# A streaming conformer encoder layer in float32: depthwise taps tied behind softmax minima, input rows asked for earlier, two FFN products exchanged, outputs on another DMA queue

## The chip, the cores and the metric

The kernel runs on one core of one Trainium2 chip. The metric is the device time of one execution in microseconds; the kernel before has a median of 3021.13 us over three runs. Five engines work side by side, each through its own instructions in their order: TensorE (PE) multiplies matrices and transposes, VectorE (DVE) and ScalarE (ACT) do elementwise work, GpSimd (POOL) some more of it, and SyncE (SP) issues nearly all DMA transfers. ACT can issue DMAs too, on a queue of its own.

## The reference, cut to what matters

A prompt of 2048 rows and a sample of 64 rows, each row 1024 wide, pass through one layer. All is float32.

```python
h = rms_norm(x, norm1_g) * (1 + sc1) + sh1
glu_a, glu_b, q, k, v, g_conv, g_attn = split(h @ w_in)
u = glu_a * sigmoid(glu_b)
conv_out = silu(layer_norm(depthwise_conv31(u) + b_dw)) @ w_conv_out
q, k = rms_norm(q), rms_norm(k)                # per head, 8 heads of 64
o = softmax(q @ k.T / 8 + bias, banded) @ v    # own chunk of 64 and 8 chunks before
merged = sigmoid(g_conv) * conv_out + sigmoid(g_attn) * (o @ w_attn_out)
x = x + gt1 * (merged @ w_o)
gate, up = split((rms_norm(x, norm2_g) * (1 + sc2) + sh2) @ w_ffn_in)
y = x + gt2 * ((silu(gate) * up) @ w_ffn_out)
```

The depthwise convolution has 31 taps per channel and reads the 30 rows before. Rows of u, k and v are returned as states too.

## The kernel before, in words

Every float32 product is made of three matmuls on halves of the operands: a high part (`whi`, `hh`) that ACT copies out and a low part (`wlo`, `hl`) that DVE or POOL makes by a subtraction.

**First phase: four row blocks.** The 2112 rows are worked in blocks of 576, 512, 512 and 512 rows (`PBLOCKS`, line 34). The table `ORDER` (line 536) gives each block eight stages: `q`, channel tile 0, `k`, tile 1, `v`, tiles 2 and 3, and the sixteen gate columns `g`. A channel tile is one call of `glu` (line 1174): PE makes two products, 48 matmuls of 512 columns in the last three blocks, ACT takes a tanh, and DVE writes `u`. Then `convolve` (line 1202) runs its 31 taps over that tile on DVE: one `tensor_scalar` with the bias, and thirty `scalar_tensor_tensor`, all writing the same `y`, so that each follows the one before. When the four tiles are through, `conv_norm` (line 1221) normalises over channels: POOL sums the four tiles into `s`, PE multiplies `s` by a matrix of ones, and DVE, ACT and POOL share the rest.

Attention of a block begins two model microseconds after its `v` stage and goes on beside tiles 2 and 3, the gates and the next block's first stages. Each head (`attend`, line 1412) makes four score tiles `sc` on PE, one per 128 rows. There is one buffer for `sc` (tag `s`, `bufs=1`; in the first block two score tiles share it, one in each half). So PE can start a score tile only when `softmax_max` (line 1314) has read the one before: that is one DVE instruction which adds the bias and takes the row minimum of the negated scores (`pr`, with its result in `sm`). ACT makes the exponentials, PE transposes them (`ptp`), ACT and DVE split them (`ph`, `pl`), and PE multiplies by v (`po`).

The next block's rows are prepared in the same phase: `norm_tile` (line 1109) loads 128 rows as `x_t`, ACT squares them, POOL takes the power, DVE scales, PE transposes (`pt<-ident,x_t`), DVE applies the modulation, and ACT and DVE write `hh` and `hl`, which the next block's products read. The generators of the four tiles are put in their lane at the twelfth gate (`NORM_G` = 11), two at a time. There are three `x_t` buffers, in a pool that also holds the rows of v on their way out.

**What sets the order.** All steps are generators in lanes (`Lane`, line 108), emitted along a model of each engine's load (`Stream`, line 161). What is emitted then goes through the framework's scheduler, which reorders each engine's instructions by readiness in a time model of its own. `issue_after(ins)` forbids it to place an instruction ahead of `ins` on the same engine.

**Second phase: merge and FFN**, in three row blocks of 576, 768 and 768 (`CBLOCKS`, line 35). The FFN's first product runs as seven half-size products per column group `f`, a recursive scheme with sums of weights and sums of activations; `up_operands` (line 540) lists the weights' order and `up` (line 1962) issues the products. The products named `s2` and `s1` go into the same PSUM bank `y`, and between them ACT must copy the bank to `u` (`u2`). In the last two row blocks the FFN's second product is cut into four parts per pair of `f` (`down_pair`, line 1938), put between the products at the places that `dn_at` (line 548) gives; in the first row block `down` (line 2022) runs between two products of every even `f`. The last `down` of a row block makes the outputs `acc`, which leave by `nc.sync.dma_start`, so on SP's queue, behind which the next row block's gate columns (`tg<-g_d`) are loaded.

Of the kernel before, what the change touches and what calls it, by code (L numbers as in the profile page):

```python
# [44 lines left out]
TURN_LAG = 2500.0  # L45
KN_LAG = 5000.0
X_LAG = 8000.0
ON_POOL = ()
DMA_LAG = 4000.0
OUT_LAG = 4000.0  # L50
# [2 lines left out]
SIDE_G = 10  # L53
SPLIT_G = 2
NORM_G = 11
NORM_W = 2
SCORE_ROOM = {"dve": 2500}
TURN_NS = 600.0
# [481 lines left out]
def up_operands(f):  # L540

    ops = (["s2", "s3", "s1"] if f else ["s3", "s2", "s1"]) + ["a12"] * (f >= EARLY) + ["a22"] + ["a11"] * (EARLY <= f + 1 < NF) + ["s4"]
    return [(f + (op == "a11"), op) for op in ops]


def dn_at(f):

    return (0, 1, 3, 6 if f == PAIRS[-1] else 4)  # L550


def mod_order():
# [34 lines left out]
def streaming_layer(ctx: ExitStack, tc: tile.TileContext, I, O):  # L588
# [512 lines left out]
    def square(x_t, n):  # L1101
# [4 lines left out]
        dve.tensor_tensor(ssq[:n, 0:1], ssq[:n, 0:1], ssq[:n, 1:2], ALU.add)  # L1106
        return rsqrt_mean(wk, ssq[:n, 0:1], n, 1, D)

    def norm_tile(lo, t, free):

        c = slice(t - lo, t - lo + P)
        x_t = load_x(t, P, wa, "x", 3)
        yield stream.load["pe"] + X_LAG
        r = square(x_t, P)
        yield stream.when("pool")
        dve.tensor_scalar(x_t, x_t, r, None, ALU.mult)
        yield stream.when("dve") + PE_LAG
        for g in range(2):
            pt = ps_g.tile([P, 4, P], F32, tag="gp", name="pt")
            h = temp("h32", (P, 4, P))  # L1120
            for k in range(4):
                pe.transpose(pt[:, k], x_t[:, (4 * g + k) * P : (4 * g + k + 1) * P], ident)
            stream.after("dve", "pe")
            for k in range(4):
                kk = 4 * g + k
                dve.tensor_scalar(h[:, k], pt[:, k], A1[:, kk, 0:1], B1[:, kk, 0:1], ALU.mult, ALU.add)
            yield stream.when("dve")
            yield lambda: free["columns"] >= c.stop
            f = slice(4 * g, 4 * g + 4)
            act.activation(hh[:, f, c], h, AF.Copy)  # L1130
            yield stream.when("act")
            dve.tensor_tensor(hl[:, f, c], h, hh[:, f, c].bitcast(F32), ALU.subtract)
# [66 lines left out]

    now = {"scored": -1, "finished": -1, "bias": None}  # L1200

    def convolve(u, y, ct, b):
        w = UW if b == 0 else HIST + QB
        n = w - HIST
        states = [(cs_s, HIST + SMP)] if b == 0 else [(cs_p, w)] if b == len(PBLOCKS) - 1 else []
        if states:
            yield stream.when("dve") + TURN_LAG
        for rows_, e in states:
            pt = ps_g.tile([P, 512], F32, tag="gp", name="pt")
            pe.transpose(pt[:HIST, :P], u[:, e - HIST : e], ident)  # L1210
            s = wa.tile([HIST, P], F32, tag="cc", name="cc", bufs=2)
            dve.tensor_scalar(s, pt[:HIST, :P], 0.5, None, ALU.mult)
            stream.at(stream.when("dve"), lambda s=s, rows_=rows_: nc.sync.dma_start(rows_[:, ct * P : (ct + 1) * P], s))
            yield
        gps.tensor_copy(hist[:, ct], u[:, w - HIST : w])
        dve.tensor_scalar(y[:, ct, :n], u[:, :n], wd[:, ct, 0:1], bdw[:, ct : ct + 1], ALU.mult, ALU.add)
        for k in range(1, TAPS):
            dve.scalar_tensor_tensor(y[:, ct, :n], u[:, k : k + n], wd[:, ct, k : k + 1], y[:, ct, :n], ALU.mult, ALU.add)
            yield

    def conv_norm(y, c0, n, t0):
        yv = y[:, :, c0 : c0 + n]
        yield lambda: not conv.gens
        s = wk.tile([P, 512], F32, tag="ln_s", bufs=1)

        def total():
# [311 lines left out]
    for b, stage in ORDER:  # L1538
        lo, hi = PBLOCKS[b]
        if stage == "q":  # L1540
            free, ahead = {"columns": 0}, {}
            if b + 1 < len(PBLOCKS):
                ahead = {t: norm_tile(hi, t, free) for t, _ in token_tiles(*PBLOCKS[b + 1])}
        if stage == "q" and b == 0:
            pass
        elif stage in ("q", "k", "v"):
            qkv(b, "qkv".index(stage), norms)
            if stage == "v":

                def heads(b=b):  # L1550
                    work.drain()
                    stream.flush()
                    attention(b)
                    if b == 3:
                        attn.burst, attn.spacing = 2, 0.0

                stream.at(stream.load["pe"] + HEADS_NS, heads)
        elif stage == "g":
            for g in gates(b, free):
                if g == NORM_G:  # L1560
                    for gen in ahead.values():
                        norm_lane.add(gen)
                if g == SIDE_G and b == len(PBLOCKS) - 1:
                    work.drain()
                    conv.drain()
                    stream.flush()
                    side.close()
                    wc = ctx.enter_context(tc.tile_pool(name="wc", bufs=1, side="right"))
                    cs = tile_chunks(*CBLOCKS[0])[0]
                    src = load_mixed(*cs, 0)  # L1570
                    first_gates = gate_columns(*cs, 0)
            norms = ahead
        else:
# [173 lines left out]
    for s, (lo, hi) in enumerate(CBLOCKS):  # L1747
# [208 lines left out]
        def rest_of_late(n=99):  # L1956
            while late and n:
                n -= 1
                if next(late[0], None) is None:
                    late.pop(0)  # L1960

        def up(f, ops, at):
# [25 lines left out]
            v = half_piece(1, "v")[:, :half]  # L1988
            keep(v, z)
            rest_of_late()  # L1990
            if f % 2 == 0:
                at(0)
            step(y, "s1", "t1", False, False)
            plus(v, y, v)
            if f % 2:
                at(4)
            if f >= EARLY:
                x = bank("gp")
                step(x, "a12", "b21", True, True)
                plus(x, x, s1)  # L2000
                silu(c1, x)
            if f % 2 == 0:
                at(1)
            step(z, "a22", "t4", False, True)
            plus(z, z, u2)
# [16 lines left out]
        def down(fs, ws):  # L2022

            last = fs[-1] == NF - 1
            for i, (t, n) in enumerate(tiles):
# [19 lines left out]
                for j, ps in enumerate(pss):  # L2045
# [9 lines left out]
                    else:  # L2055
                        if not final:
                            dve.tensor_tensor(ps[:m], ps[:m], both, ALU.add)
                        if n < m:
# [5 lines left out]
                        dve.tensor_tensor(dst, ps[:n], dst if final else x1[j], ALU.add)  # L2064
                        stream.at(
                            stream.when("dve") + OUT_LAG,
                            lambda t=t, n=n, f=f, dst=dst: nc.sync.dma_start(rows(y_p, y_s, t, n)[:, f], dst),
                        )
            for _ in fs:
                W.done()  # L2070
# [91 lines left out]
```

## Time and profile before

| | |
|---|---|
| median of three runs | 3021.13 us (3019.73 to 3027.58) |
| the profiled execution | 3021.16 us |
| its span, first to last instruction | 3018.7 us |
| mean granted TensorE clock | 0.987 of full speed |
| PE, DVE, ACT, POOL busy | 96%, 67%, 44%, 32% of the span |
| DMA moved | 690.95 MB, mean 229 GB/s |
| row blocks of the first phase end at about | 345, 640, 930 and 1222 us |
| merge and FFN, three row blocks, end at about | 1735, 2377 and 3019 us |

The time of an execution lies about 2.5 us over its span. A wait is told as who sat idle, for how long, and whose result ended it. Instructions of the kernel's engines all carry line 103, which is the recording helper, so they are told apart by the tiles that they write and read: `sc` are scores, `sm` the minima and sums, `y<-u,wd,y` a tap, `ps` a product's bank.

### The profile page before, as it was taken

How to read it: one execution, taken by the hardware profiler on the slowest of the kernel's cores; microseconds unless marked ns; L12 is line 12 of the kernel's file. 1: busy time of each engine (PE TensorE's matmuls, PEld its weight loads, DVE VectorE, ACT ScalarE, POOL GpSimd, SP SyncE). 2: the span in 40 equal slices, each digit the busy share in tenths (PEclk: the TensorE clock that was granted, in tenths of full speed). 3: DMA queues.
4: the chain of work that ended last, by engine and by line, in shares of the span. 5: the costliest groups of instructions: out<-in, count | busy, mean ns of one | idle time of the engine just before them, and what ended most of it. 6: DMA issues, size and time to landing. Idle time of an engine off the chain costs nothing. (4 is left out here: it accounts for less than half of the span.)

```text
span 3018.7 us, 44690 instructions
## 1 busy us (share of the span) xinstructions
PE 2912.8 (96%) x16199; PEld 2600.1 (86%) x16199; DVE 2019.5 (67%) x3647; ACT 1324.5 (44%) x2375; POOL 956.4 (32%) x599
## 2 busy tenths in 40 slices
PE   7989898999999999999999999999999999999998
PEld 4889776888878788888999989999999898999997
DVE  5896687657966895577766755556565757366567
ACT  3334542563355256464444335434444244333331
POOL 1200120101011101355467323157766331333331
PEclk9999999999999999999999999999999999999999
DMA  9888888887987789886444786446556965355554
GB/s 301 266 279 284 264 293 292 265 255 259 305 273 223 254 284 295 256 295 235 149 146 155 240 286 223 151 141 202 194 170 212 352 206 188 116 168 175 168 163 174
DMA packets 487018, 690.95 MB, mean 229 GB/s; under 512 B 38421, under 2 KB 316809, under 8 KB 486798
## 3 DMA queue, kind: packets, MB, share of 16 engines
q1 hardware_dynamic: 474517, 670.72, 67.8%
q10 hardware_dynamic: 12280, 17.39, 1.6%
q8 instruction: 127, 2.08, 0.3%
q14 instruction: 94, 0.76, 0.1%
HBM read 503.79 MB, written 184.19 MB: 228 GB/s over the span
## 5 line engine op out<-in xcount | busy, mean ns | idle before, releaser
L103 POOL TENSOR_TENSOR wlo<-wst,whi 128x1024 fp32r<-128x1024 f32 (+1 forms) x171 | 388.1, 2274 | 495.3 <-ACT whi L103 448.5
L103 PE MATMUL ps<-t,whi 128*128 128x384 f32 (+1 forms) x2112 | 507.2, 324 | 12.4 <-DVE t L103 5.5
L103 PE MATMUL pd<-whi,hid 128*128 128x512 f32 x1356 | 439.7, 391 | 3.4 <-DVE acc L103 3.4
L103 ACT ACTIVATE whi<-wst 128x1024 fp32r<-128x1024 f32 (+1 forms) x272 | 265.7, 980 | 346.2 <-PE ps L103 117.3
L103 PEld LDWEIGHTS ps<-t,whi 128*128 128x128 f32 x2112 | 371.4, 189 | 21.2 <-DVE t L103 6.4
L103 PE MATMUL ps<-b,whi 128*128 128x384 f32 (+1 forms) x1584 | 379.9, 325 | 1.9 <-DVE pt L103 1.6
L103 DVE SCALAR_TENSOR_TENSOR y<-u,wd,y 128x512 f32<-128x512 f32 (+1 forms) x480 | 369.0, 773 | 8.2
L103 PE MATMUL ps<-hh,whi 128*128 128x512 f32 (+2 forms) x992 | 363.1, 366 | 0.3 <-DVE pl L103 0.3
L103 PE MATMUL ps<-hl,whi 128*128 128x512 f32 (+2 forms) x992 | 345.7, 348 | 0.0
L103 PE MATMUL ps<-hh,wlo 128*128 128x512 f32 (+2 forms) x992 | 345.7, 348 | 0.0
L103 PE MATMUL ps<-t,wlo 128*128 128x384 f32 (+1 forms) x1056 | 341.0, 323 | 0.0
L103 DVE TENSOR_TENSOR acc<-acc,pd 128x512 f32<-128x512 f32 x440 | 289.7, 683 | 69.8 <-PE pd L103 65.9
L103 PEld LDWEIGHTS pd<-whi,hid 128*128 128x128 f32 x1356 | 254.5, 188 | 57.8 <-DVE acc L103 6.5
L103 PEld LDWEIGHTS ps<-b,whi 128*128 128x128 f32 x1584 | 277.0, 189 | 4.9 <-DVE pt L103 2.0
L103 PE MATMUL pd<-wlo,hid 128*128 128x512 f32 x700 | 273.7, 391 | 0.0
L103 PE MATMUL ps<-b,wlo 128*128 128x384 f32 (+1 forms) x792 | 256.3, 324 | 0.0
L103 ACT ACTIVATE pr<-pr,sm 128x640 f32<-128x640 f32 (+3 forms) x272 | 200.0, 747 | 127.6 <-DVE sm L103 125.7
L103 POOL TENSOR_TENSOR r<-t,mhalf 128x1 f32<-128x1 f32 (+3 forms) x68 | 82.3, 1212 | 417.5 <-DVE t L103 373.2
L103 PEld LDWEIGHTS ps<-hh,wlo 128*128 128x128 f32 x992 | 187.4, 189 | 22.7 <-issue 0.4
L103 PEld LDWEIGHTS ps<-hh,whi 128*128 128x128 f32 x992 | 188.0, 190 | 19.3 <-issue 2.7
L103 PEld LDWEIGHTS ps<-hl,whi 128*128 128x128 f32 x992 | 188.2, 190 | 15.5 <-issue 1.7
L103 PEld LDWEIGHTS ps<-t,wlo 128*128 128x128 f32 x1056 | 199.6, 189 | 0.6
(218 smaller groups left out, 5663.0 us busy)
## 6 DMA issues: line engine op xcount, KB each, us to landing
whi<-w_din_h SPq DMA_DIRECT2D x72, 512.0 KB, 4.0
wlo<-w_din_l SPq DMA_DIRECT2D x72, 512.0 KB, 7.3
wst<-sum_d SPq DMA_DIRECT2D x131, 256.0 KB, 2.9
wmod<-in_w_ada SPq DMA_DIRECT2D x48, 512.0 KB, 6.9
sum_d<-ws SPq DMA_DIRECT2D x88, 256.0 KB, 2.2
wst<-in_w_ffn_in SPq DMA_DIRECT2D x85, 256.0 KB, 3.4
wst<-in_w_in SPq DMA_DIRECT2D x40, 512.0 KB, 7.4
wst<-in_w_ffn_in SPq DMA_DIRECT2D x37, 512.0 KB, 5.5
```

Source lines behind the costliest of these rows:

```text
L103: return f(*args, **kw)
```

## The change

It has five parts.

1. **Taps behind minima.** `softmax_max` already keeps its last instruction in `now["least"]`. In the first three blocks each tap now takes that instruction out, if one has been emitted since the last tap, and is itself emitted under `issue_after`: the scheduler may no longer place it, nor the taps after it, which need its result, ahead of that minimum. Taps of the fourth block are emitted as before.
2. **Channel norm later.** `conv_norm` of the first three blocks waits, once the taps are emitted, for another 10000 ns of the model's PE time (`MEAN_LAG`).
3. **Input rows earlier.** The load of `x_t` is taken out of the generator: at the fourth gate (`ROWS_G` = 3) three tiles are asked for at once, and the fourth when the first has been transposed.
4. **FFN order.** For odd `f` from 5 on, product `a12` is issued ahead of `s1` instead of behind it; the last of the four parts of `down_pair` moves from place 4 to place 5, which is still right behind `s1`.
5. **Outputs on ACT's queue.** The stores of `acc` are issued by `nc.scalar` instead of `nc.sync`.

```diff
+MEAN_LAG = 10000.0
+ROWS_G = 3
...
-    ops = (["s2", "s3", "s1"] if f else ["s3", "s2", "s1"]) + ["a12"] * (f >= EARLY) + ["a22"] + ["a11"] * (EARLY <= f + 1 < NF) + ["s4"]
+    ops = (["s2", "s3"] if f else ["s3", "s2"]) + ["a12"] * (f >= EARLY and f % 2) + ["s1"] + ["a12"] * (f >= EARLY and f % 2 == 0) + ["a22"] + ["a11"] * (EARLY <= f + 1 < NF) + ["s4"]
...
-    return (0, 1, 3, 6 if f == PAIRS[-1] else 4)
+    return (0, 1, 3, 6 if f == PAIRS[-1] else 5)
...
+    def ask(t):
+        if t not in asked:
+            asked[t] = load_x(t, P, wa, "x", 3), stream.load["pe"] + X_LAG
...
-        x_t = load_x(t, P, wa, "x", 3)
-        yield stream.load["pe"] + X_LAG
+        ask(t)
+        x_t, landed = asked.pop(t)
+        yield landed
...
+            if g and t + 3 * P < lo + QB:
+                ask(t + 3 * P)
...
+    def behind(one):
+        return tc.issue_after(one.ins) if one is not None else nullcontext()
...
         for k in range(1, TAPS):
-            dve.scalar_tensor_tensor(y[:, ct, :n], u[:, k : k + n], wd[:, ct, k : k + 1], y[:, ct, :n], ALU.mult, ALU.add)
+            with behind(now.pop("least", None) if b < 3 else None):
+                dve.scalar_tensor_tensor(y[:, ct, :n], u[:, k : k + n], wd[:, ct, k : k + 1], y[:, ct, :n], ALU.mult, ALU.add)
...
         yield lambda: not conv.gens
+        if t0 < PBLOCKS[-1][0]:
+            yield stream.load["pe"] + MEAN_LAG
...
             for g in gates(b, free):
+                if g == ROWS_G:
+                    for t in list(ahead)[:3]:
+                        ask(t)
...
             if f % 2 == 0:
                 at(0)
+            else:
+                factor()
             step(y, "s1", "t1", False, False)
             plus(v, y, v)
             if f % 2:
-                at(4)
-            if f >= EARLY:
-                x = bank("gp")
-                step(x, "a12", "b21", True, True)
-                plus(x, x, s1)
-                silu(c1, x)
-            if f % 2 == 0:
+                at(5)
+            else:
+                factor()
                 at(1)
...
-                            lambda t=t, n=n, f=f, dst=dst: nc.sync.dma_start(rows(y_p, y_s, t, n)[:, f], dst),
+                            lambda t=t, n=n, f=f, dst=dst: nc.scalar.dma_start(rows(y_p, y_s, t, n)[:, f], dst),
```

The new function `factor` holds the lines of `a12` that are taken out above, its `bank`, `step`, `plus` and `silu`.

DVE where the second row block's first head begins (`y<-u,wd,y` are taps, `ISA pr,sm<-sc,bias` a minimum, `u<-tb,ps` the end of channel tile 2, `R` and `A` small work of the modulation). Before:

```order
L103 SCALAR_TENSOR_TENSOR u<-tb,ps 128x512
L103 TENSOR_SCALAR y<-u,wd,cols 128x512
L103 COPY R<-pa 128x256
L103 SCALAR_TENSOR_TENSOR y<-u,wd,y 128x512 x4
L103 TENSOR_TENSOR A_173<-pa,cols 128x2x2x2
L103 SCALAR_TENSOR_TENSOR y<-u,wd,y 128x512
L103 TENSOR_TENSOR A_173<-A_173,cols 128x2x2x2
L103 SCALAR_TENSOR_TENSOR y<-u,wd,y 128x512 x15
L103 ISA pr,sm<-sc,bias 128x640
L103 ISA sm 128x1
L103 SCALAR_TENSOR_TENSOR y<-u,wd,y 128x512 x2
```

The same place now:

```order
L105 SCALAR_TENSOR_TENSOR u<-tb,ps 128x512
L105 TENSOR_SCALAR y<-u,wd,cols 128x512
L105 COPY R<-pa 128x256
L105 TENSOR_TENSOR A_173<-pa,cols 128x2x2x2
L105 TENSOR_TENSOR A_173<-A_173,cols 128x2x2x2
L105 ISA pr,sm<-sc,bias 128x640
L105 ISA sm 128x1
L105 RECIPROCAL sm<-sm 128x1
```

The twenty taps between tile 2 and the first minimum are gone from there; behind the row shown last the other three minima follow without a tap between them, and the taps come after the fourth.

DVE where the fourth row block's first head begins (`vst` are rows of v). Before:

```order
L103 TENSOR_TENSOR vst<-ps,vst 128x4x128
L103 SCALAR_TENSOR_TENSOR y<-u,wd,y 128x512 x4
L103 ISA pr,sm<-sc,bias 128x640
L103 ISA sm 128x1
L103 RECIPROCAL sm<-sm 128x1
```

The same place now:

```order
L105 TENSOR_TENSOR vst<-ps,vst 128x4x128
L105 SCALAR_TENSOR_TENSOR y<-u,wd,y 128x512 x5
L105 SCALAR_TENSOR_TENSOR u<-tb,ps 128x512
L105 TENSOR_SCALAR y<-u,wd,cols 128x512
L105 SCALAR_TENSOR_TENSOR y<-u,wd,y 128x512 x7
L105 ISA pr,sm<-sc,bias 128x640
L105 ISA sm 128x1
L105 SCALAR_TENSOR_TENSOR y<-u,wd,y 128x512 x2
```

Here, where nothing is tied, tile 2's `u` and eight of its taps (one of them the `tensor_scalar`) have moved ahead of the first minimum, and two more stand between the first and the second. On PE the four score tiles of this head, which had 3 to 6 product matmuls between them, now stand in one row of sixteen matmuls, behind the 24 matmuls of the next `glu` product.

SP where the second block's input rows are loaded, in the first block's gate stage (`o_d` are attention's results, `c_d` those of the convolution). Before, the first two of the four loads:

```order
L1371 DMA o_d<-part_h 128x64
L1371 DMA o_d<-part_l 128x64
L1098 DMA x_t<-in_x_prompt 128x1024
L1275 DMA c_d<-part_h 128x64
L1275 DMA c_d<-part_l 128x64
L1098 DMA x_t<-in_x_prompt 128x1024
```

Now, the first three of the four:

```order
L1366 DMA vv<-v_d 128x4x128
L1390 DMA o_d<-part_h 128x512
L1390 DMA o_d<-part_l 128x512
L1100 DMA x_t<-in_x_prompt 128x1024 x3
L383 DMA wst<-in_w_in 128x4x256
L487 DMA w_din_1_h<-whi 128x1024
```

The three loads stand 56 rows of SP's list earlier than the first of them did, behind an attention store of the first heads; the fourth stays near the place where the third and fourth were.

More of the change, by code (lines that the diff above doesn't have):

```diff
@@ L1107, in square @@
         return rsqrt_mean(wk, ssq[:n, 0:1], n, 1, D)
+    asked = {}
+    def ask(t):
+        if t not in asked:
+            asked[t] = load_x(t, P, wa, "x", 3), stream.load["pe"] + X_LAG
     def norm_tile(lo, t, free):
         c = slice(t - lo, t - lo + P)
-        x_t = load_x(t, P, wa, "x", 3)
-        yield stream.load["pe"] + X_LAG
+        ask(t)
+        x_t, landed = asked.pop(t)
+        yield landed
         r = square(x_t, P)
@@ L1990, in up, with factor @@
             rest_of_late()
+            def factor():
+                if f >= EARLY:
+                    x = bank("gp")
+                    step(x, "a12", "b21", True, True)
+                    plus(x, x, s1)
+                    silu(c1, x)
             if f % 2 == 0:
                 at(0)
+            else:
+                factor()
             step(y, "s1", "t1", False, False)
```

## The prediction

> **What bounds the kernel now.** I read the page's busy times first, then a table by stage, then who PE waits for.
>
> ```profile
> PE 2912.8 (96%) x16199; PEld 2600.1 (86%) x16199; DVE 2019.5 (67%) x3647; ACT 1324.5 (44%) x2375; POOL 956.4 (32%) x599
> ```
>
> PE is the bound, with 3018.7 - 2912.8 = 105.9 us of idle time. The table by stage (columns: length, busy time of PE, PEld, DVE, ACT, POOL, granted clock, DMA share, GB/s) shows where that lies; its rows are the four row blocks of the first phase and the second FFN block.
>
> ```profile
> 180.00:345.00 165.00, 152.82 (x1089) 145.14 (x1088) 121.23 (x256) 85.98 (x204) 15.31 (x22) 0.97 0.85 276
> 345.00:640.00 295.00, 270.72 (x1428) 219.27 (x1427) 208.22 (x422) 133.72 (x262) 37.94 (x35) 0.96 0.88 287
> 640.00:930.00 290.00, 283.09 (x1593) 236.75 (x1594) 209.29 (x407) 138.47 (x251) 31.36 (x30) 1.00 0.84 266
> 930.00:1222.00 292.00, 286.91 (x1493) 242.03 (x1492) 218.65 (x414) 154.27 (x274) 39.38 (x29) 0.99 0.80 254
> 1777.00:2345.00 568.00, 565.41 (x2958) 526.63 (x2957) 331.23 (x569) 257.46 (x426) 306.49 (x174) 1.00 0.56 187
> ```
>
> The idle time is in blocks one and two (12.2 and 24.3 us), and the clock is below 1 there as well. From 1777 us on PE is idle for 2.6 of 568 us: the new order of the FFN products can win next to nothing in the last two row blocks. Among PE's waits, these are the groups that the change could touch (columns: total us, count, the longest):
>
> ```profile
> PE sc L103 <- DVE sm L103: 20.8, 11, 10.1
> PE pt L103 <- DVE x_t L103: 9.4, 6, 3.6
> PE sc L103 <- DMA kk<-k_d: 7.6, 5, 2.7
> PE ps L103 <- DVE part_l L103: 1.3, 1, 1.3
> PE ps L103 <- DVE pl L103: 0.3, 1, 0.3
> PE ps L103 <- ACT u L103: 3.3, 6, 0.6
> ```
>
> **Term 1: the second block's first head.** The timeline of PE and then of DVE:
>
> ```profile
> 493.63 0.80 PE L103 MATMUL sc<-kk,q 128*128 128x320 f32 x4
> 504.56 1.43 PE L103 MATMUL sc<-kk,q 128*128 128x320 f32 x4 [10.12 <-DVE sm L103]
> 506.92 1.43 PE L103 MATMUL sc<-kk,q 128*128 128x320 f32 x4 [0.93 <-DVE sm L103]
> 509.28 1.43 PE L103 MATMUL sc<-kk,q 128*128 128x320 f32 x4 [0.93 <-DVE sm L103]
> ...
> 953.53 1.27 PE L103 MATMUL sc<-kk,q 128*128 128x320 f32 x4 [2.07 <-DMA kk<-k_d]
> ...
> 491.99 11.78 DVE L103 SCALAR_TENSOR_TENSOR y<-u,wd,y 128x512 f32<-128x512 f32 x15
> ```
>
> The scores lay ready at 494.4; DVE had fifteen taps (11.78 us, so 0.79 each) queued ahead of the minimum. In the new order no tap stands between tile 2 and the four minima. What stays is the ping-pong over the one `sc` buffer, about 0.93 a tile as in the two rows that follow: say 2.3 us in place of 10.12 + 0.93 + 0.93 = 11.98. That wins 9.7. The clock comes on top; the windows that hold its low stretches:
>
> ```profile
> 189.00:199.40 10.40, 5.07 (x15) 3.42 (x16) 9.30 (x21) 3.38 (x11) 0.00 (x0) 0.51 0.35 132
> 359.70:370.00 10.30, 6.38 (x17) 4.09 (x18) 7.27 (x20) 6.06 (x12) 3.00 (x4) 0.50 1.07 283
> 499.70:513.40 13.70, 6.99 (x23) 5.57 (x23) 11.77 (x25) 5.99 (x12) 0.00 (x0) 0.50 0.45 155
> 953.60:957.10 3.50, 3.50 (x10) 2.98 (x11) 3.44 (x8) 1.39 (x3) 0.00 (x0) 0.51 0.00 0
> ```
>
> PE worked 6.99 us at half clock after this gap, which at full clock is 3.5; I take 2.3 of the 3.5, because the last row shows a half-clock stretch after a gap of only 2.07 us (953.53, above), and 2.3 us remain here. Term 1: **-12.0** (bounds -14 and -9). [...]
>
> **Term 2: the first block's first heads.** PE, and the DVE row ahead of the minimum:
>
> ```profile
> 193.54 0.80 PE L103 MATMUL sc<-kk,q 128*128 128x256 f32 x2 [5.70 <-DVE sm L103]
> ...
> 187.12 6.16 DVE L103 SCALAR_TENSOR_TENSOR y<-u,wd,y 128x606 f32<-128x606 f32 x7
> ```
>
> In the new order three taps stand where these seven do, and five more have gone from ahead of the `u` before them. Three at 0.88 end at about 189.8, so 5.70 becomes about 1.7: -4.0. Of the half-clock work, 5.07 / 2 = 2.5, I take 1.5. Term 2: **-5.5** (-8 to -2).
>
> **Term 3: the first block's input rows for the second.** PE at the seam, and the four loads among the `x_t` instructions of 290 to 380 us:
>
> ```profile
> 326.55 0.63 PE L103 MATMUL pt<-ident,x_t 128*128 128x128 f32 x4 [1.57 <-DVE x_t L103]
> ...
> 356.39 0.47 PE L103 MATMUL po<-ph,vv 128*128 128x512 f32 x1 [1.85 <-DMA vv<-v_d]
> 360.74 1.97 PE L103 MATMUL pt<-ident,x_t 128*128 128x128 f32 x8 [3.64 <-DVE x_t L103]
> 366.36 0.80 PE L103 MATMUL ps<-whi,hh 128*128 128x512 f32 x1 [2.14 <-ACT hh L103]
> ...
> L1098 SPq DMA_DIRECT2D x_t<-in_x_prompt x4: 422/423/495, 314.1 to 353.6; - x4
> ```
>
> The fourth load is issued at 353.6, between products that need its rows a few microseconds on. Now three are issued some 100 us ahead (behind an attention store of the first heads, by SP's list) and the fourth when the first tile is through. I expect the waits of 3.64 and 2.14 to go and the 1.57 of the first row, which is of the same kind, with them: 7.3 less. Of the half-clock work, 6.38 / 2 = 3.2, I take 1.7. Waits for `vv`, as the 1.85, may stay. The three loads are 1.5 MB, some 5.5 us at the 276 GB/s of that stage, pushed ahead of weight loads; PE shows no wait for a weight there, so I cost them at nothing, and at 5 us if that cover is gone. Term 3: **-9.0** (-13 to -2).
>
> **Term 4: the fourth block's first head, a new wait.** Before, PE waited for its minima hardly at all:
>
> ```profile
> 1059.99 0.82 DVE L103 CUSTOM_DVE_ANT_0 pr<-sc,bias 128x640 f32<-128x640 f32 x1 [2.23 <-PE sc L103]
> ...
> 1064.68 0.69 DVE L103 SCALAR_TENSOR_TENSOR u<-tb,ps 128x512 f32<-128x512 f32 x1
> 1065.40 0.55 DVE L103 TENSOR_SCALAR y<-u,wd,cols 128x512 f32<-128x512 f32 x1
> ```
>
> Here DVE waited 2.23 us for the scores. Now the scores come 24 matmuls (5.5 us, at 0.23 each: half the 0.47 of the row at 356.39, which ran at half clock) after the product that `u` needs, and DVE must first do `u` (0.69), the first tap (0.55) and seven taps (7 x 0.78 = 5.4): 6.6 us, then the minimum. The first score tile ends at 5.5 + 0.8 = 6.3; the second starts at 7.6, the third, two taps and a minimum later, at 10.1, the fourth at 11.8. PE idles 1.3 + 1.6 + 0.9 = 3.8 us, with some of a half-clock stretch behind it: **+5.0** (+2, if the list absorbs it, to +10, if it becomes what block two was).
>
> **Term 5: `a12` ahead of `s1`.** PE, in the first FFN block, one of six such rows:
>
> ```profile
> 1684.97 0.53 PE L103 MATMUL ps<-t,whi 128*128 128x288 f32 x2 [0.55 <-ACT u L103]
> ```
>
> Product `s1` waits for ACT's copy, which is behind `hid` on ACT. Twelve matmuls of `a12` (1.6 us) now cover the 0.55. The next thing late would be `a22` on ACT's copy `v`, which is done 1.3 us before that product could now start. Six times 0.55: **-3.3** (-4 to 0). In the last two row blocks the rows are full already: 0, with +-1.
>
> **Term 6: outputs on ACT's queue.** SP at the first FFN seam, then PE:
>
> ```profile
> 1744.64 7.42 SPq L2067 DMA_DIRECT2D out<-acc  x10
> 1752.15 1.79 SPq L1085 DMA_DIRECT2D tg<-g_d  x2
> ...
> 1757.80 0.59 PE L103 MATMUL ps<-cin,whi 128*128 128x384 f32 x2 [1.55 <-DVE t L103]
> 1762.64 0.59 PE L103 MATMUL ps<-cin,whi 128*128 128x384 f32 x2 [0.24 <-DVE t L103]
> 1766.33 0.62 PE L103 MATMUL ps<-cin,whi 128*128 128x384 f32 x2 [1.24 <-DVE m L103]
> ```
>
> The gate columns stood behind ten stores for 7.4 us, and PE then idled 1.55 + 0.24 + 1.24 = 3.0. Half of it is won: **-1.5** (-3 to 0). On ACT eight of the ten stores now stand ahead of the next weight copy. ACT had been idle for 17.88 us when it made that copy:
>
> ```profile
> 1737.29 1.06 ACT L103 ACTIVATE whi<-wup 128x1024 fp32r<-128x1024 f32 x1 [17.88 <-PE pd L103]
> ```
>
> So I cost the stores there at nothing, and at 1 us for each of the two seams if one of them holds the copy up. [...]
>
> **Term 7: what the rest costs.** The 29 taps taken from ahead of minima (9 x 0.88 + 20 x 0.78 = 23.5 us) must run later, between the `pl` subtractions that PE waits for, and the channel norm ends later. No row shows what that costs; the nearest, in the groups above, are the one wait for `pl`, 0.3, and the one for the norm's `part_l`, 1.3. A stall of 1.0 in each of three blocks, between these two, gives **+3**; the bounds are -2 (both gone, 1.6) and +8 (six such waits of 1.3 for each of three blocks would be 23; I take a third).
>
> **The sum.** -12.0 - 5.5 - 9.0 + 5.0 - 3.3 - 1.5 + 3.0 = -23.3, against the profiled execution's 3021.16 (span 3018.7 and 2.5 around it; the median of the runs, 3021.13, is the same): **2998 us**.
>
> **The rivals.**
>
> *The rows don't come earlier in effect.* Transfers share of the DMA engines is 0.85 to 0.88 in blocks one and two; if the early rows only push weights and keys back by as much, term 3 is 0: 3007. Against it: 100 us of lead. Chance 0.10.
>
> *The taps' stalls are moved, not removed.* DVE is busy 208 to 219 of about 292 us per block, but in the stretch of four channel tiles nearly all the time; if the 23.5 us of taps reappear as late `u` and `pl`, terms 1 and 2 cancel and 3 and the others give -9 - 3.3 - 1.5 + 5 + 3 = -6: 3015. Chance 0.13.
>
> *Slower: DVE waits for scores that are late.* A tap behind a minimum can't fill DVE's time while a head's key load is late, and whatever is queued behind it waits too: the rest of that tile's taps, then `u`, then PE.
>
> ```profile
> 855.80 0.83 PE L103 MATMUL sc<-kk,q 128*128 128x320 f32 x4 [2.73 <-DMA kk<-k_d]
> ```
>
> If the earlier row loads and the moved stores of attention bring such a wait to eight heads of the first three blocks, and each costs 2.73 and half of a half-clock stretch like the 3.50 quoted, that is 8 x (2.73 + 1.75) = 36 us on top of the forecast: 3034. Five such heads, 22 us, eat the forecast's gain; it decides from eight on. For it: keys are already the third group of PE's waits. Against it: five waits of 7.6 us in all, and a mean idle share of DVE of a quarter that can take them. Chance 0.11.
>
> *The change does not do what it says* would be that the scheduler places taps ahead of the minima as before; the order of DVE in the second block rules that out, and it is only in the first block that three taps are left.
>
> **How the numbers follow.** Forecast 2998, chance 0.66; rows pushed back, 3007, 0.10; stalls moved, 3015, 0.13; late scores, 3034, 0.11. A measurement of this kernel can tell about 0.3%, 9 us, from no change, so faster means under 3012 and slower over 3030. The forecast's own range comes from the half-widths of the seven terms, 2.5, 3, 5.5, 4, 2, 1.5 and 5, taken as independent: the root of their squares is 9.6, and since most bounds reach further toward a loss I say 2987 to 3010. To hold 8 in 10 the range goes on to the two middle rivals: 2984 to 3016. Faster: forecast and first rival, less 0.02 for a forecast that ends over 3012, 0.74; same: the second rival and those 0.02, 0.15; slower 0.11.
>
> **What would show it right or wrong.** Term 1: no row of fifteen taps on DVE at about 492, gaps of under 1 us before each score tile of block two's first head, no half-clock stretch behind. Term 2: 5.70 falls to under 2. Term 3: the first three `x_t` loads are issued at about 220 to 255, and no `x_t` or `hh` wait over 1 us stands at the seam of 345 to 370; if weights or keys take their place, the first rival is true. Term 4: waits `sc<-sm` of 1 to 2 us at the fourth block's first head, near 1060. Term 5: the six `u` waits of 0.5 are gone and none for `v` has come. Term 6: no stores on SP near 1745, and `tg` loads some 7 us earlier. Term 7: PE's waits for `pl`, `u` of the channel tiles and `part_l` stay under 3 us together; if they reach 20, the second rival is true. The forecast is wrong if blocks one and two are not shorter by some 25 us together, or if block three, where taps are now tied though its idle time was 6.9 us of 290, grows longer than it was.

## The result, and the profile after

| | median | range | profiled span | mean clock |
|---|---|---|---|---|
| before | 3021.13 us | 3019.73 to 3027.58 | 3018.7 | 0.987 |
| changed | 3009.85 us | 3009.00 to 3012.74 | 3008.0 | 0.987 |

Both medians are of five runs. The ratio of the changed kernel's runs to those of the kernel before is 0.9958, with a 95% interval of 0.9945 to 0.9970. That is a gain of 12.7 us (9 to 17), about half of the 23 that were forecast; the time lies inside the range of 2984 to 3016.

The page's row of busy times, which stood at 2912.8 for PE:

```profile
PE 2919.7 (97%) x16199; PEld 2603.0 (87%) x16199; DVE 2029.9 (67%) x3671; ACT 1323.1 (44%) x2375; POOL 915.9 (30%) x575
```

PE's idle time fell from 105.9 to 3008.0 - 2919.7 = 88.3 us, so by 17.6. But the same 16199 matmuls kept PE busy for 6.9 us longer. Worked out from the records of the granted clock, the work that PE did in stretches at half clock was 52.9 us before and is 61.3 now, which costs 4.2 us of the 6.9 in these two executions.

Where the time came from is read from waits that stand in both traces at the same instruction: the first product of the first merge, and that of the third. Before, and then in the changed kernel:

```profile
1225.33 0.53 PE L103 MATMUL ps<-cin,whi 128*128 128x320 f32 x2 [2.66 <-DVE row L103]
...
2377.26 0.62 PE L103 MATMUL ps<-cin,whi 128*128 128x384 f32 x2 [0.55 <-DVE acc L103]
```

```profile
1214.95 0.87 PE L105 MATMUL ps<-cin,whi 128*128 128x320 f32 x2 [2.67 <-DVE row L105]
...
2362.28 0.62 PE L105 MATMUL ps<-cin,whi 128*128 128x384 f32 x2 [0.55 <-DVE acc L105]
```

The whole first phase won 10.4 us. The two merge and FFN blocks up to 2377 us brought that to 15.0, and the rest gave 4.3 back, since the spans differ by 10.7. PE's waits of the changed kernel, with the groups that were shown of before and those that grew:

```profile
PE sc L105 <- DVE sm L105: 14.0, 11, 2.8
PE ptp L105 <- ACT pr L105: 9.1, 10, 2.1
PE pt L105 <- DVE x_t L105: 4.4, 3, 1.5
PE sc L105 <- DMA kk<-k_d: 3.5, 2, 2.1
...
PE ps L105 <- DVE m L105: 2.9, 2, 2.5
...
PE ps L105 <- ACT hh L105: 0.6, 2, 0.3
```

The waits for `x_t`, `kk` and `hh` shrank as forecast, and those of 3.3 for ACT's `u` have no row any more. But the waits for minima fell from 20.8 by only 6.8, and those for exponentials (`ptp` behind ACT's `pr`, 2.1 in two waits before) are 9.1 in ten. In block two's first head the fifteen taps are gone and PE's idle time fell nearly as far as forecast, though a half-clock stretch of 6.83 us stayed. PE, and then DVE where the taps stood:

```profile
499.74 0.82 PE L105 MATMUL sc<-kk,q 128*128 128x320 f32 x4 [1.40 <-DMA kk<-k_d]
501.84 1.44 PE L105 MATMUL sc<-kk,q 128*128 128x320 f32 x4 [1.28 <-DVE sm L105]
504.20 1.43 PE L105 MATMUL sc<-kk,q 128*128 128x320 f32 x4 [0.93 <-DVE sm L105]
...
500.95 0.82 DVE L105 CUSTOM_DVE_ANT_0 pr<-sc,bias 128x640 f32<-128x640 f32 x1 [4.94 <-DMA bias<-rb_d]
503.31 0.82 DVE L105 CUSTOM_DVE_ANT_0 pr<-sc,bias 128x640 f32<-128x640 f32 x1 [0.38 <-PE sc L105]
```

Now DVE waits: at the first tile for the bias, which by the profile came 0.39 us after the scores, and then for scores. The four tiles lose 3.6 us in place of 12.0. The new waits for minima are 3.8 us at block four's first head, told below, and 6.4 us in block one's last heads, beside block two's first stages. DVE and then PE there:

```profile
393.77 0.69 DVE L105 SCALAR_TENSOR_TENSOR ln<-ln,y 128x512 f32<-128x512 f32 x1
394.38 0.69 DVE L105 TENSOR_TENSOR part_l<-ln,part_h 128x512 fp32r<-128x512 f32 x1
...
395.35 0.69 DVE L105 SCALAR_TENSOR_TENSOR u<-tb,ps 128x512 f32<-128x512 f32 x1
...
399.10 0.55 DVE L105 CUSTOM_DVE_ANT_0 pr<-sc,bias 128x384 f32<-128x384 f32 x1
...
399.72 0.72 PE L105 MATMUL sc<-kk,q 128*128 128x512 f32 x2 [2.76 <-DVE sm L105]
```

PE had these scores ready at 395.81. From then until 399.10 DVE was busy with tile 0's `u`, its first taps and a copy. They came so late because the channel norm's steps (`ln`, `part_l`) stood ahead of them: the tanh that `u` needs was done at 391.71.

### The profile page after: what moved, and what is told of

It reads as the page before. It is cut to its first block, busy times and chain, and to the rows that moved or that the text cites. A ratio compares the mean times of both kernels' runs of the same rounds, so it can differ in the third digit from the quotient of the medians.

```text
span 3008.0 us, 44650 instructions
## 1 busy us (share of the span) xinstructions
PE 2919.7 (97%) x16199; PEld 2603.0 (87%) x16199; DVE 2029.9 (67%) x3671; ACT 1323.1 (44%) x2375; POOL 915.9 (30%) x575
## 4 chain that ended last, share of the span: by engine, by line
PE 84%; DVE 7%; DMA 5%; issue 1%; ACT 1%; POOL 1%; SPq 0%; ACTq 0%; DVEq 0%; POOLq 0%
PE ps L105 55%; PE pd L105 14%; PE pw L105 6%; PE po L105 2%; PE sc L105 2%; DVE y L105 2%; PE ptp L105 2%; PE pt L105 1%; DMA cin<-o_d 1%; DVE wlo L105 1%; PE pa L105 1%; POOL r L105 1%; DVE pr L105 1%; DMA tg<-g_d 0%; DMA x<-x_d 0%
## 5 line engine op out<-in xcount | busy, mean ns | idle before, releaser
L105 PEld LDWEIGHTS ps<-t,whi 128*128 128x128 f32 x2112 | 370.8, 189 | 17.5 <-DVE t L105 7.4
```

The source lines that it names most:

```text
L105: return f(*args, **kw)
```

## The experiments

All were timed beside the kernel before on the same chip. The ratio is to those runs, with its 95% interval, and the last column is the ratio's distance from 1 times 3021 us.

| kernel | median | ratio | in us |
|---|---|---|---|
| ties alone | 3014.66 | 0.9977 (0.9963 to 0.9991) | -6.9 |
| earlier rows alone | 3016.23 | 0.9974 (0.9965 to 0.9984) | -7.9 |
| FFN order alone | 3019.25 | 0.9986 (0.9977 to 0.9994) | -4.2 |
| outputs on ACT alone | 3028.91 | 1.0019 (1.0010 to 1.0028) | +5.7 |
| the change | 3009.85 | 0.9958 (0.9945 to 0.9970) | -12.7 |
| ... with outputs on SP | 3009.27 | 0.9948 (0.9936 to 0.9960) | -15.7 |
| ... without ties | 3016.39 | 0.9974 (0.9965 to 0.9984) | -7.9 |
| ... block four tied too | 3016.12 | 0.9968 (0.9956 to 0.9980) | -9.7 |
| ... ties in two blocks only | 3013.64 | 0.9963 (0.9950 to 0.9977) | -11.2 |
| ... norm not delayed | 3002.20 | 0.9926 (0.9914 to 0.9938) | -22.4 |
| ... delay for the sample only | 3004.28 | 0.9931 (0.9919 to 0.9944) | -20.8 |
| ... no ties, no delay | 3011.00 | 0.9956 (0.9942 to 0.9970) | -13.3 |
| ... no delay, outputs on SP | 2999.07 | 0.9918 (0.9905 to 0.9930) | -24.8 |

**Each part alone.** First the ties: the kernel before with this.

```diff
-            dve.scalar_tensor_tensor(y[:, ct, :n], ...)
+            with behind(now.pop("least", None) if b < 3 else None):
+                dve.scalar_tensor_tensor(y[:, ct, :n], ...)
```

> The kernel before with the first part alone: taps of blocks one to three tied behind minima. Theory (the ties win at the first heads and give some of it back in new small waits): in block one's first heads PE's idle time falls by about 4.6 us, before block two's second score tile by about 8.4, as in the full change; block four's first head gets its new wait of about 4 us; and PE's waits for exponentials (ptp <- ACT pr, 2.1 us in two waits before, 9.1 in ten in the full change) rise to 6 us or more. Time: about 3016. Rival (the waits for exponentials come from the earlier input rows): those waits stay near 2 us, and the time is about 3010.

Measured: -6.9 us. The theory's 3016 was close and its account half wrong. The waits for exponentials did not come with the ties (2.9 us), and block four's first head got no wait at all. What did come is POOL's sum:

```profile
PE pm L103 <- POOL s L103: 7.0, 3, 5.6
...
PE sc L103 <- DVE sm L103: 6.0, 7, 1.9
...
PE ptp L103 <- ACT pr L103: 2.9, 5, 1.7
```

At block two's first head PE waits 1.96 us in place of 11.98. So the ties take 14.8 us out of the waits for minima and put 7.0 of waits for the channel norm's sum `s` in their place, since the last taps end later and PE's product with the ones stands in its list ahead of that.

The earlier rows alone (`ask`, `ROWS_G` and their calls, as in the diff of the change):

> The kernel before with the third part alone: input rows asked for earlier. Theory: the seam of 345 to 370 us loses its waits for x_t and hh, 7 us of idle time, and its half-clock stretch of 10.24 us, with one or two short ones in their place; key waits at 853 and 951 us (2.73 and 2.07) go too, as in the full change, because the loads of rows no longer stand ahead of the keys; waits for exponentials stay near 2 us. Time: about 3010. Rival (the gain of block three, some 8 us, comes from the ties): the key waits at 853 and 951 stay, and the time is about 3015.

Measured: -7.9 us, between the two. At the seam of 340 to 420 us the waits for `x_t` are gone and one for `hh` of 0.6 is left; in their place PE waits once for the norm's sum, 3.0 us:

```profile
PE pm L104 <- POOL s L104: 3.0, 1, 3.0
...
PE ps L104 <- ACT hh L104: 0.6, 1, 0.6
```

Between 930 and 1045 us nothing waits for keys any more, which the kernels without this part all did (1.84 to 2.37 us at some 950 us). The wait near 853 us proves nothing: it is absent from the profile of the outputs alone too, a kernel that differs only behind 1700 us. And this part alone brings the wait at block four's first head that I had put down to the ties. PE there, with the earlier rows alone, and then with the ties alone:

```profile
1054.20 0.85 PE L104 MATMUL sc<-kk,q 128*128 128x320 f32 x4 [0.93 <-DVE sm L104]
1056.40 1.43 PE L104 MATMUL sc<-kk,q 128*128 128x320 f32 x4 [1.34 <-DVE sm L104]
```

```profile
1052.06 0.74 PE L103 MATMUL sc<-kk,q 128*128 128x320 f32 x4
1054.03 0.74 PE L103 MATMUL sc<-kk,q 128*128 128x320 f32 x4
```

The order of the FFN products alone (`up_operands`, `dn_at` and `up`):

> The kernel before with the fourth part alone: a12 ahead of s1 for odd f from 5 on. Theory: the six waits of 0.55 us for u go, and the one of 1.04 for s at 1466 us, 4.3 in all, and nothing changes in the two last row blocks; waits for v (1.17 and 0.48 in the full change, near 1370 and 1392 us) come from elsewhere and stay away. Time: about 3016.5. Rival (the new order brings the waits for v): 1.7 less of a gain, about 3018.5.

Measured: -4.2 us, as the theory said. The waits for `u` and `s` have no row left, and the stretch of 1413 to 1734 us, 321 long with 316.63 of PE's work before, is full. The waits for `v` do stand in this profile (1.6 us), as in those of every kernel here but the one before, the outputs alone among them: from 1330 to 1413 us the kernels compared lose 2.5 to 3.7 us against the profile of before, those that change nothing there too. The profile of before holds an execution with fewer waits in that stretch than the others have. A term of under 4 us can't be read from one pair of profiles here.

The outputs alone:

```diff
-                            lambda t=t, n=n, f=f, dst=dst: nc.sync.dma_start(rows(y_p, y_s, t, n)[:, f], dst),
+                            lambda t=t, n=n, f=f, dst=dst: nc.scalar.dma_start(rows(y_p, y_s, t, n)[:, f], dst),
```

> The kernel before with the fifth part alone: outputs issued on ACT's queue. Theory: the first seam of the FFN row blocks gains about 3 us (PE's 3.0 us of waits there go), and the second loses about 4.6, because ACT holds its weight copies and the copy m behind eight stores, each waiting for its sum: PE gets a wait for m of about 2.5 us and a half-clock stretch of 3.4. Time: about 3022.7. Rival (the wait at the second seam comes from another order of SP's loads there in the full change): the first seam's 3 us alone, 3018.

Measured: +5.7 us (3 to 8.5), a loss. The second seam loses as the theory said, and the first, where 3.0 us should have been won, wins nothing. ACT at the second seam, then what SP waits for there:

```profile
2367.59 12.23 ACTq L2067 DMA_DIRECT2D out<-acc  x8
2380.76 1.06 ACT L103 ACTIVATE whi<-wst 128x1024 fp32r<-128x1024 f32 x1 [16.92 <-PE pd L103]
...
2392.95 1.06 ACT L103 ACTIVATE whi<-wup 128x1024 fp32r<-128x1024 f32 x1 [11.13 <-DMA wup<-in_w_attn_out]
```

```profile
SPq L381 <- DMA cin<-c_d: 5.5, 2, 3.0
SPq L1093 <- DMA out<-acc: 5.3, 2, 3.3
SPq L381 <- DMA cin<-o_d: 2.7, 1, 2.7
```

The first weight copy is no later than before, as its idle time of 16.92 us, which ends on PE, is the same in both. It is the second that waits, 11.13 us, for weights that SP loads late, and SP is late because it waits for the stores. In the traces of before and after all DMAs signal on eight semaphores, and each of the eight carries DMAs of SP (1906 in all before, 1872 now) and of ACT (94 and 128). In each of the two, 1982 of the 1992 DMAs that follow another on the same semaphore were issued when that one had landed. So a store that stands on ACT until its sum is there holds one of the eight, and a load on SP that needs it stands too, with all that is queued behind it: the 5.3 us above. PE then waits 1.92 us for `m` and runs 3.41 us at half clock.

**The change with one thing undone.** Outputs back on SP's queue:

> The changed kernel with the stores of acc back on SP's queue. Theory (stores on ACT cost time: they stand ahead of ACT's weight copies, and SP's loads come to wait for them, 5.9 us at the second seam of the FFN row blocks): the 5.7 us that the fifth part cost alone come back, the waits for m of 2.55 us at 2375 us and for out<-acc on SP go; time about 3004.5. Rival (in the full change the first seam's gain of 2.9 us belongs to these stores, so that they cost only 1.7 in sum): about 3008.

Measured: ratio 0.9948 beside 0.9958, so 3.0 us better; the intervals overlap, but the trace has it at its place. SP's first waits at that seam are now for weight copies, none for stores, and PE's wait for `m` at 2375 us is gone:

```profile
SPq L383 <- DVE wlo L105: 4.4, 2, 2.7
SPq L1095 <- PE pd L105: 3.7, 2, 1.8
```

The first seam loses 2.0 us by it, the second wins 4.5, by the starts of the same products in the two traces. So the stores cost some 3 us in this setting, between the theory's 5.7 and the rival's 1.7, and the intervals exclude neither.

Ties left out (`with behind(...)` taken away):

> The changed kernel without the ties (taps of all blocks emitted as in the fourth). Theory (the parts add up, and the ties are worth 7 us): about 3016.5; PE's waits for minima return to 20 us or more, block two's second score tile alone waiting some 10 us, and the waits for exponentials fall from 9.1 to 4 or 5. Rival (with the early rows and the later channel norm the ties are worth their forecast 12 + 5.5): 3024 or more. Either way block four's first head keeps its three waits of about 1 us, since the earlier rows alone showed them too.

Measured: 3016.39 us, ratio 0.9974; beside 0.9958 the ties are worth 4.8 us. The waits for minima are back at 24.9 us and those for exponentials at 4.4. The wait of block two's second score tile is 7.8 us, and block four's first head keeps its three waits (1.02, 1.34 and 0.93).

Ties in block four too:

```diff
-            with behind(now.pop("least", None) if b < 3 else None):
+            with behind(now.pop("least", None) if b < 4 else None):
```

> The changed kernel with the taps of block four tied as well. Theory (the wait at block four's first head is the ping-pong over the one score buffer, because the four score tiles now stand in one row on PE; two taps less between two minima win little): the waits of 1.50, 1.34 and 0.92 us become three of about 0.93, and the time falls by 1 us or nothing, 3009. Rival (the forecast's reading: taps ahead of the minima make it): the waits and the half-clock stretch at 1057 us go, and the time is about 3004.5.

Measured: 0.9968, so no gain over 0.9958; the intervals overlap. The waits became three of 0.92 or 0.93, two of them shown, as the theory said, but the first tile now waits for its key:

```profile
1056.56 0.87 PE L105 MATMUL sc<-kk,q 128*128 128x320 f32 x4 [1.94 <-DMA kk<-k_d]
1058.36 1.44 PE L105 MATMUL sc<-kk,q 128*128 128x320 f32 x4 [0.93 <-DVE sm L105]
1060.72 1.43 PE L105 MATMUL sc<-kk,q 128*128 128x320 f32 x4 [0.93 <-DVE sm L105]
```

With no product between the score tiles, 0.93 us a tile is what one `sc` buffer costs in these traces, whoever stands behind the minima.

The channel norm's delay at zero:

```diff
-MEAN_LAG = 10000.0
+MEAN_LAG = 0.0
```

> The changed kernel with the channel norm's extra delay at zero. Theory (the taps that are moved behind the minima end later, and without the delay PE's product with the ones stands in its list before POOL's sum s is there, as with the ties alone, where PE waited 7.0 us in three waits): waits for s of 5 us or more return, and the time is about 3014. Rival (the delay does nothing, since the earlier rows move the list anyway): 3010, and no wait for s over 1 us.

Measured: 3002.20 us, ratio 0.9926: the theory fell, and so did the rival. The wait for `s` came back as expected, 8.6 us, and the kernel is still 9.7 us faster than with the delay. What goes is larger: over the whole trace PE's waits for minima and exponentials fall from 23.1 to 10.0 us. Most of that goes between block one's last heads. PE's waits from 370 to 445 us with the delay, and then without:

```profile
PE sc L105 <- DVE sm L105: 6.3, 4, 2.8
PE ptp L105 <- ACT pr L105: 3.3, 3, 1.9
```

```profile
PE sc L105 <- DMA kk<-k_d: 2.1, 1, 2.1
PE ps L105 <- DMA wlo<-w_dqkv_l: 1.4, 1, 1.4
```

Delayed by 10 model us for the sample's rows and by 10 more for the 512 rows behind them, block one's norm lands on DVE between the minima of block one's last heads (the rows at 394 above), where it pushes `u` and taps ahead of a minimum that PE waits for. Ahead of them it costs PE one wait of 7.26 us. The waits don't account for the whole gain: new ones for keys take back 2.5 us, PE's idle time falls by only 1.6 in all, and most of the 5.8 by which the span is shorter stands in the profile as less busy time. Where that comes from is not shown.

**What the delay and the ties have to do with each other.** The delay for the sample's rows alone:

```diff
-        if t0 < PBLOCKS[-1][0]:
+        if t0 == 0:
             yield stream.load["pe"] + MEAN_LAG
```

> The changed kernel with the channel norm's delay kept only for the sample's 64 rows, the first norm of block one. Theory (without any delay PE waited 7.26 us for the sample's sum s; with it everywhere, the norm of block one's 512 rows lands between block two's minima, where PE waits 2.76, 1.35 and 0.89 us for minima and 1.94 for exponentials): both go, and the time is 6 us under the kernel with no delay, about 2996. Rival (one delay is enough to push the norm behind it, in the same lane, into block two's minima): waits for minima of some 5 us near 375 to 440 us remain, and the time is that of the changed kernel, 3008 to 3012.

Measured: 0.9931 beside 0.9926, no different from no delay at all. The theory and the rival both failed in part: the wait of 7.26 us is gone, and so are the waits for minima, but from 370 to 445 us PE waits 3.4 us for a key and 2.1 for exponentials, and over the whole trace 8.8 us for exponentials.

Neither ties nor delay:

> The changed kernel without the ties and with no delay of the channel norm, so the earlier rows, the FFN order and the outputs alone. Theory (the ties are worth their forecast, but only when the norm isn't delayed): about 3016, by the sum of the three parts measured alone, 14 us over the kernel with ties and no delay. Rival (the delay costs its 8 to 10 us with or without ties): 3008, since the kernel with the delay and without ties had 3016.

Measured: 0.9956, between the two. Without the delay the ties are worth 0.9956 - 0.9926, 9.1 us; with it 4.8. The delay costs 9.7 us with the ties and 5.4 without. So the delay is a loss with the ties and, less surely, without them. That the two get in each other's way is not shown: the 4 us between these differences lie within the four intervals.

No delay, and the outputs on SP:

> The changed kernel with no delay of the channel norm and with the outputs back on SP's queue. Theory (the two costs add): 3 to 5 us under the kernel with no delay alone, 2998. Rival (the outputs on ACT cost nothing that the next stage doesn't hide, as the seams with no delay suggest, which lose 2.2 and 1.3 us but win at the first seam): 3002.

Measured: 2999.07 us, ratio 0.9918 (0.9905 to 0.9930), the fastest of all: 12 us under the changed kernel by the ratios. The outputs' share of it, 2.4 us, lies within the intervals and where the theory had it, at the second seam.

Last, block three's part of the ties:

```diff
-            with behind(now.pop("least", None) if b < 3 else None):
+            with behind(now.pop("least", None) if b < 2 else None):
```

> The changed kernel with the ties in blocks one and two only. Theory (block three had nothing to win from ties: before the change PE waited there for keys, hh and R, 7 us in all, and hardly for minima, and it is the earlier rows that take those waits away, as the kernel with the earlier rows alone showed): the time is that of the changed kernel within 2 us, 3010 to 3012 beside a kernel before of 3021 to 3024, a ratio of 0.995 to 0.997. Rival (the 8 us that block three gained in the changed kernel come from its ties): the key waits near 850 and 950 us come back, ratio 0.998 or more.

Measured: 0.9963, as the theory said: the tie of block three is worth 1.5 us, which the intervals can't tell from nothing. Without it, PE still waits for no key near 850 and 950 us.

## Why the prediction was right, and its gain nearly twice the measured one

The sign and the range held. The terms, one by one:

- **Terms 1 and 2, the first heads: right in mechanism, too large by their clock.** The idle time went from 11.98 to 3.61 us in block two (I had 2.3 left; 1.40 of the 3.61 is a wait for a key) and from 9.65 to 5.01 in block one's stretch of 185 to 266 us. But of the half clock 3.8 us were to come back in these two places and 0.7 did: PE's work at half clock went from 6.95 to 5.13 us and from 5.00 to 5.46. In the changed kernel with the outputs on SP, which differs only behind 1700 us, it is 2.99 and 5.42, so 1.8 came back there.
- **Term 3, the rows: right as a whole, at other places.** The forecast was -9.0, all at block one's seam; measured alone it is -7.9. In the changed kernel the three waits of 7.35 us are gone from the seam, with 1.70 for `hl`, the low part that goes with `hh`, and 0.32 for `hh` in their place. With the rows alone the seam lost 3.0 us to a sum that nobody waited for before, block three won a key wait that I had not counted, and block four's first head lost what I had booked as term 4. All kernels here with the earlier rows, and none without, also wait 2.06 to 2.09 us for exponentials near 270 us.
- **Term 4: the size right (5.0 forecast; the three waits are 3.76 us, where I had 3.8, and 3.41 us at half clock behind them cost 1.7), the cause wrong.** I read it from the untied list of the changed kernel and put it down to the ties ending at block three. The earlier rows alone show it, the ties alone don't, and tying block four doesn't take it away. The list showed what stood there, but not which part of the change had put it there. The row of 0.47 us that I took for half clock ran at full clock, since the low stretch begins at 359.76; matmuls of 512 columns do follow each other at 0.23 us there.
- **Term 5: right.** -3.3 forecast, -4.2 measured (-6.9 to -1.8).
- **Term 6: the sign wrong.** The step that failed was "So I cost the stores there at nothing": I followed ACT's list at the first seam only, and not the loads on SP that share semaphores with the stores. -1.5 was forecast; it costs 5.7 us alone and about 3 in the change. In the new traces SP's issues do stand behind the stores' transfers, in waits for `out<-acc` of 5.3 us alone and 5.9 in the change.
- **Term 7: mis-sized.** I gave +3 to everything that comes later and worked the price out from the taps. The delay of the channel norm alone costs 9.7 us. I had not asked where on DVE the norm's work lands, though the parts were in the diff.

Terms 6 and 7 were off by some 4.5 and 6.7 us, 11 in all, about the whole difference between -23.3 and -12.7. The kernel without the delay and with the outputs on SP is at -24.8, and the forecast's remaining five terms sum to -24.8. That does not show these five to be right: it is luck, with an interval of 8 us around the measured one and errors that cancel. Terms 1 and 2 sum to -17.5, where the ties are worth 9.1 us without the delay. The earlier rows and the FFN order measured alone sum to -12.1, where terms 3, 4 and 5 sum to -7.3.

The prediction's own sign for blocks one and two, shorter by some 25 us together, failed. ACT's tanh for the third block's first channel tile starts at 693.7 us before and at 684.6 now. From 177.4 us (178.9 now) to there, PE's idle time fell from 39.1 to 25.4 us. At the places that terms 1 to 3 name, it fell by 8.4, 4.6 and 5.3 us, 18.3 of the 21.0 booked; waits beside them took a net 4.6 back, the new ones for minima and exponentials from 268 to 440 us above all. From there to the fourth block's first tile, where nothing was booked, it fell from 6.5 to 0.6.

Of the rivals, the second (stalls moved, not removed) came half true, with another carrier: in the changed kernel it is the norm behind the 23.5 us of taps that lands on other minima. Without the delay the norm's sum takes part of the ties' gain: PE waits 8.6 us for `s` in the kernel with ties and no delay, and not at all in the one with neither. The first was wrong, the rows did come earlier. SP's four loads in the changed kernel:

```profile
L1100 SPq DMA_DIRECT2D x_t<-in_x_prompt x4: 333/436/478, 245.7 to 350.4; - x4
```

The first is issued at 245.7 us, where it was 314.1. The third stayed away: keys cost PE 3.5 us in the changed kernel, where they cost 7.6.

## What to carry to other kernels

When work is pushed off one critical place, find the place where it lands in the list and who waits there, before pricing the push; a model's delay of 10 us cost more than the wait that it removed. A DMA that is moved to another engine's queue is not alone there: here the stores on ACT shared their semaphores with the loads on SP, which came to wait 5.3 us for them with the outputs alone and 5.9 in the change. And a change of five parts is read part by part: four runs with one part each and three with one part undone showed that two of the five were losses.

## What the runs showed of the hardware

In the traces of before and after the half clock came in stretches of 3.41, 6.83, 10.24 and 13.65 us, whole multiples of 3.413, but for the last of each, which the end of the trace cuts off. In each of the two the starts of the stretches lie on one grid, whole multiples of 3.413 us apart: those at 499.7 and 953.7 us before by 133 of them. A wait of 2 to 3 us brought a stretch in some places and none in others. The same wait of the last FFN block, 2.42 us before and 2.40 in the changed kernel, with the windows of the grid around it, and in the kernel before the stretch behind it (busy times of PE, PEld, DVE, ACT, POOL, clock):

```profile
2539.88 0.44 PE L103 MATMUL ps<-t,whi 128*128 128x384 f32 x1 [2.42 <-DVE t L103]
...
2537.47:2540.88 3.41, 1.00 (x6) 1.00 (x7) 3.41 (x6) 1.53 (x2) 0.08 (x1) 1.00 0.61 204
...
2540.90:2544.20 3.30, 3.30 (x12) 3.23 (x11) 3.30 (x6) 1.08 (x2) 0.00 (x0) 0.50 0.48 141
```

```profile
2529.45 0.45 PE L105 MATMUL ps<-t,whi 128*128 128x384 f32 x1 [2.40 <-DVE t L105]
...
2525.17:2528.59 3.42, 1.88 (x11) 1.55 (x9) 3.42 (x3) 2.42 (x4) 1.95 (x1) 1.00 0.46 149
2528.59:2532.00 3.41, 2.53 (x13) 2.21 (x13) 3.41 (x7) 1.58 (x3) 0.00 (x0) 1.00 0.84 287
```

Before, the wait falls into one window, in which PE is busy for 1.00 of 3.41 us, and half clock follows. In the changed kernel it lies across two windows, PE is busy for 1.88 and 2.53 us of them, and none follows. From 120 us on, up to 30 us before the end, these two traces hold 20 windows at full clock with half clock behind them, and PE is busy for 0.00 to 1.51 us in each of these; in the other 1624 it is busy for 1.55 us or more. That is a count of two executions and gives no threshold: over all fourteen traces half clock follows 13 of the 49 windows in which PE is busy for 45% to 57%, 1.54 to 1.95 us. What sets the clock is not shown. In the changed kernel a wait of 1.90 us at 297 us, inside one window with PE busy for 1.51 us, had a stretch of 6.83 behind it, and one of 2.76 at 397 us, across two with 1.71 and 2.36, had none.

Counted from the first instruction, the starts lie 1.36 us past whole multiples of 3.413 in the profile of before and 2.72 past them in that of the changed kernel. Executions of one kernel differ in their clock too: the 30 runs of the kernel before that stand beside the parts alone have mean clocks of 0.985 to 0.991. The outputs alone change nothing before 1700 us; yet from 178 to 697 us that kernel has 37.6 us of idle time and 30.4 of work at half clock, where the kernel before has 39.1 and 18.3. Less idle time did not mean less work at half clock: PE's idle time fell by 17.6 us with the change while its work at half clock grew by 8.4, though in the changed kernel with the outputs on SP that work is 51.9 us, no more than before.
